# Experts of a two-layer backbone: split token rows, paired scatters, no dummy products, an eighth raw buffer

## The chip, the cores and the metric

The kernel runs on one core of a Trainium2 chip. The time is device microseconds from launch to end of one execution; several executions give a median. TensorE is called PE, VectorE DVE, ScalarE ACT, GpSimd POOL; SP is the engine that issues the loads of the weights.

## The reference

The program is a two-layer backbone for 256 tokens of width 1024. Each layer mixes tokens (short convolution, gated chunks, windowed attention) and then channels. Layer 0's channel mixer is dense; layer 1's is a mixture of experts, which is where the change lies:

```python
def moe_swiglu(h, router, w_gu, w_d):
    logits = jnp.einsum("bld,de->ble", h, router, preferred_element_type=jnp.float32)
    top_v, top_i = lax.top_k(logits, TOP_K)          # 2 of 8 experts for a token
    top_w = jax.nn.softmax(top_v, axis=-1)
    gates = jnp.sum(jax.nn.one_hot(top_i, N_EXPERTS, dtype=jnp.float32) * top_w[..., None], axis=-2)
    y = gates[..., 0:1] * swiglu(h, w_gu[0], w_d[0])
    for e in range(1, N_EXPERTS):
        y = y + gates[..., e:e + 1] * swiglu(h, w_gu[e], w_d[e])
    return y                                          # then x + g2 * y, and a last RMSNorm
```

An expert is 3584 wide: `w_gu[e]` is 1024 x 7168 and `w_d[e]` 3584 x 1024, all fp32.

## The kernel before, in words

**Products in fp32.** Where many tokens share a weight, both factors are split in a high and a low part of a rounded fp32 type (fp32r), and three products high-high, low-high and high-low take the place of one fp32 product. The tile framework records the program in the order of the code, engine by engine, and puts semaphore waits where tiles are shared.

**The token rows.** Ahead of the experts, `token_scale` makes the normalised and modulated rows `tm` (128 tokens x 2 halves x 1024) in four quarters of 512 columns: DVE multiplies from PSUM, POOL adds the shift in place. Between the second and the third quarter DVE works out the tokens' ranks. For an expert, `prep_p` makes a selection matrix P with one 1 a column (its slots: up to 128 for a full block, 64 more on the side), `prep_x` gathers the tokens as products `tm` x P of 192 columns into X (full block, split again in `Xe`; side in `Xo`), `prep_g` scales P by the gates and `prep_t` transposes it for the way back. Expert 0's gather runs ahead of the first weights, those of the others between steps.

**Steps and chunks.** An expert has seven steps of 512 hidden columns, and a table `steps` mixes up to LANES = 3 experts. One step is seven turns of PE: four chunks of gate and up weights (`products`, into PG and PU), the transposition of the gated result (`turned`), two chunks of down weights (`down`, into PY). A chunk is 128 x 2048 fp32, 1 MB, and each is loaded by SP into one of seven raw buffers (raw0 to raw3, mraw, and raw2 and raw4 of the pool `mp`); a load is issued once the buffer's last reader is done.

**Branches by the token counts.** `modes` writes three variants of every turn: full (a 128-token block, 12 split products of 512 columns a chunk), the 64-wide side (fp32 straight from the raw chunk), the 32-wide side. PE reads the counts `full_` and `half_` from registers and branches. With the inputs here experts 0 and 1 have a full block and no side, expert 4 a full block and a 32-wide side, the others only a side. Where a full block has no side, the Else of the inner If issues `idle`: one 8-column product of zeros into the bank of the side. The first eight steps of the table are of experts 0 and 1; their other six alternate with side-only steps.

**Between the steps.** `items` is a table of slots, three a step (`item(3n)` and `item(3n + 1)` ahead of `down`, `item(3n + 2)` behind it), in which one piece of preparation or of scattering is issued. `scatter` brings an expert's result back to the tokens: products of the transposed selection with Y (full) and YO (side) into a bank, which DVE adds to `xt`. In the kernel before a scatter is one token half and one column half, four to an expert.

Of the kernel before, what the change touches and what calls it, by code (L numbers as in the profile page):

```python
# [18 lines left out]
D = 1024  # L19
# [7 lines left out]
NE = 8  # L27
# [109 lines left out]
def backbone_kernel(ctx, tc, xT, small, const, moe_const, gmw, gmb, modk, modd, wa, wg2, wg4, wo, fgu, fd, mgu, mdn, fing, out):  # L137
# [773 lines left out]
    cnt = mo.tile([128, 25], I32, name="cnt")  # L911
    none = mo.tile([128, 8], BF16, name="none")
    before, every = [scr(BF16)[:, 0:128] for _ in range(2)]
    nc.gpsimd.memset(none, 0.0)
    nc.gpsimd.memset(every, 1.0)
# [114 lines left out]
    def prep_p(e):  # L1030

        P = mp.tile([128, 2, NX], F32, name="P")
# [25 lines left out]
    def prep_g(e, bank=None):  # L1058
        P = X[e]["P"]
        for i in range(2):  # L1060
            nc.gpsimd.tensor_scalar(P[:, i, :], P[:, i, :], gates[:, i, e:e + 1], None, op0=OP.mult)  # L1061

    def prep_t(e, bank):

        P = X[e]["P"]
        for s in range(2):
            for i in range(2):
                nc.tensor.transpose(bank[:, s * NX + i * 128:s * NX + (i + 1) * 128], P[:, i, s * 128:(s + 1) * 128], ident)
        X[e]["T"] = pt = mp.tile([128, 2, NX], F32, name="Pt", bufs=LANES + 1)
# [38 lines left out]

    def scatter(e, i, g, bank):

        pt = X[e]["T"]
        ts, gs, hs = slice(i * 128, (i + 1) * 128), slice(g * 512, (g + 1) * 512), slice(64 * g, 64 * g + 64)

        def go(first, last):
            mm(bank, pt[:, 0, ts], X[e]["Y"][:, gs], start=first, stop=last)

        def go_o(first, last):
            mm(bank, pt[hs, 1, ts], X[e]["YO"][hs], start=first, stop=last)  # L1118

# [6 lines left out]
        with c.Else():  # L1126
            go_o(True, True)
        a = xt[:, i, gs]
        post.append(lambda: nc.vector.tensor_tensor(a, a, bank, op=OP.add))  # L1129

    def idle(bank):
        mm(bank[0:8, 0:8], none, none, start=True, stop=True)

    def modes(e, full, half, quarter=None, bank=None):

# [66 lines left out]
    def products(e, j, po):  # L1202
# [25 lines left out]
        modes(e, go, go_o, go_q, po)  # L1228

# [23 lines left out]
    def turned(e, t, po):  # L1253
# [9 lines left out]
        modes(e, turn, turn_o, None, po)  # L1263
        hh, hl = [mp.tile([128, 512], F32R, name=nm) for nm in ("hh", "hl")]
# [8 lines left out]
    def down(e, s, h3):  # L1273
# [4 lines left out]
        for j in range(2):  # L1278
# [22 lines left out]
            modes(e, go, go_o, go_q, PYO)  # L1301
            st.free()


    def scatters(e):
        return [lambda bank, i=i, g=g: scatter(e, i, g, bank) for i in range(2) for g in range(2)]

# [3 lines left out]
    def prep_back(e):  # L1311
        return [lambda bank: prep_g(e), lambda bank: prep_t(e, bank)]

    place(0, [prep_back(0)[0]])
    free = place(3, [prep_back(0)[1]])
    for e in range(1, NE):
# [3 lines left out]
        free = place(max(begin, free), prep(e) + prep_back(e))  # L1320
    for n in range(NE * NS):
        d, ds = steps[n]
        if ds == (NS if d < NE - 1 else TOGETHER) - 1:
            place(3 * n + 5, scatters(d))
    nc.gpsimd.memset(moe_scr("to"), 0.0)
# [38 lines left out]
    def spill(e):  # L1364
        P = mp.tile([128, 2, 64], F32, name="P")
        for i in range(2):
            nc.vector.tensor_scalar(P[:, i, :], slots[:, 0:64], float(SLOTS), rank[:, i, e:e + 1], op0=OP.add, op1=OP.is_equal)
        xs, pt = room[:, :, 0:64], moe_scr("tp")[:, :NX]
        po = PO[0]
        for d in range(KD):  # L1370
            for i in range(2):
                mm(po[:, 0:64], tm[:, i, d * 128:(d + 1) * 128], P[:, i, :], start=i == 0, stop=i == 1)
            nc.vector.tensor_copy(xs[:, d, :], po[:, 0:64])
        for i in range(2):
            mm(po[0:64, 0:1], P[:, i, :], gates[:, i, e:e + 1], start=i == 0, stop=i == 1)
        gs = mp.tile([128, 2], F32, name="gs")
        nc.vector.tensor_copy(gs[0:64, 0:1], po[0:64, 0:1])
        for i in range(2):
            nc.tensor.transpose(PT[0:64, i * 128:(i + 1) * 128], P[:, i, :], ident)
        nc.vector.tensor_copy(pt[0:64, :], PT[0:64, :NX])  # L1380
# [6 lines left out]
        for s in range(NS):  # L1387
# [18 lines left out]
        y, t = [moe_scr(nm) for nm in ("tg", "to")], moe_scr("tu")  # L1406
        for g in range(2):
# [12 lines left out]

    for g in range(2):
        for i in range(2):
            scatter(NE - 1, i, g, (PU, PT, PG, PO[0])[2 * i + g])
        run_post()


    ss = tiny()
    for g in range(2):
# [118 lines left out]
```

## Time and profile before

| what | value |
| --- | --- |
| median of 3 runs | 2087.51 us (2086.2 to 2089.84) |
| profiled execution | 2096.31 us, of which the span of its instructions 2094.2 |
| PE busy | 1922.0 us, 92% of the span |
| DVE, ACT, POOL busy | 62%, 33%, 21% |
| HBM read | 500.55 MB, 240 GB/s over the span |
| PE's mean granted clock | 0.962 of full speed |

The profiled execution is 8.8 us longer than the median of the timed runs. The span falls in a front part up to about 1050 us (layer 0, and layer 1's token mixing), a change-over up to 1088.5 (the router, the token rows, expert 0's gather), the steps up to 2071, and the last norm. Shares over the whole span mix these; the rows below are by stage.

### The profile page before, as it was taken

The numbers are of one execution on the slowest core, as the hardware profiler recorded it, in microseconds if no ns is written. First come the engines' busy times: TensorE is split into PE (matmuls) and PEld (weight loads), VectorE is DVE, ScalarE is ACT, GpSimd is POOL, SyncE is SP. The second block draws the span as 40 slices with busy tenths as digits, with TensorE's granted clock in tenths as the row PEclk, the third lists the DMA queues.
The fourth block names the chain that finished last, engine by engine and source line by source line (L and its number), as shares of the span: only waits on it lengthen the run. The fifth ranks groups of instructions, "written<-read, shape, count | busy, mean of one in ns | idle before, by whom it ended". The sixth has DMA issues, their size and how long they took to land. (4 is left out here: it accounts for less than half of the span.)

```text
span 2094.2 us, 31796 instructions
## 1 busy us (share of the span) xinstructions
PE 1922.0 (92%) x9396; PEld 1304.7 (62%) x9396; DVE 1300.0 (62%) x1946; ACT 695.6 (33%) x903; POOL 445.9 (21%) x188
## 2 busy tenths in 40 slices
PE   7999889989999889899989999998999998898676
PEld 4777668878888668788987765644444444332122
DVE  7488789759967772766568866654454545442222
ACT  4334332332212212554546654433232322210000
POOL 4432234233443325524420000000000000000000
PEclk9999999999999989899999999999999999999888
DMA  6323134424444553433638989999899998899995
GB/s 265 117 67 122 51 126 161 156 90 171 154 148 173 178 192 130 154 104 106 232 123 284 323 304 365 343 376 416 323 370 354 360 365 337 332 389 408 403 387 206
DMA packets 79401, 506.04 MB, mean 242 GB/s; under 512 B 8784, under 2 KB 9424, under 8 KB 28880
## 3 DMA queue, kind: packets, MB, share of 16 engines
q1 hardware_dynamic: 79056, 501.64, 64.1%
q8 instruction: 193, 3.16, 0.6%
q14 instruction: 152, 1.25, 0.2%
HBM read 500.55 MB, written 1.05 MB: 240 GB/s over the span
## 5 line engine op out<-in xcount | busy, mean ns | idle before, releaser
L106 POOL TENSOR_TENSOR w0l<-raw,w0h 128x2048 fp32r<-128x2048 f32 (+6 forms) x43 | 156.0, 3628 | 242.2 <-ACT w0h L102 222.6
L106 POOL TENSOR_TENSOR w1l<-raw,w1h 128x2048 fp32r<-128x2048 f32 (+6 forms) x42 | 153.2, 3649 | 229.4 <-ACT w1h L102 215.5
L1221 PE MATMUL PO<-raw,Xo 128*64 128x512 f32 x768 | 186.3, 620 | 11.3 <-issue 10.0
L226 DVE CUSTOM_DVE_ANT_0 scr<-mraw,crows 128x512 f32<-128x512 f32 x128 | 165.3, 1292 | 40.7 <-DMA mraw<-in_modd_dram 40.6
L1061 POOL TENSOR_SCALAR P<-P,gates 128x256 f32<-128x256 f32 x16 | 22.1, 1392 | 758.4 <-PE PO L1048 622.0
L226 DVE CUSTOM_DVE_ANT_0 scr<-mraw,crows,mcol 128x512 f32<-128x512 f32 x128 | 161.1, 1259 | 4.6
L102 ACT CAST w1h<-raw 128x2048 fp32r<-128x2048 f32 (+3 forms) x82 | 142.2, 1735 | 43.4 <-PE mm L447 22.6
L102 ACT CAST w0h<-raw 128x2048 fp32r<-128x2048 f32 (+3 forms) x82 | 141.2, 1721 | 41.9 <-PE mm L447 28.8
L446 PE MATMUL mm<-Hh,w0h 128*128 128x512 f32 (+1 forms) x380 | 139.1, 376 | 10.7 <-ACT Hh L384 4.2
L446 PE MATMUL mm<-Hh,w1h 128*128 128x512 f32 (+1 forms) x384 | 137.1, 368 | 8.9 <-ACT w1h L102 7.1
L447 PE MATMUL mm<-Hl,w0h 128*128 128x512 f32 (+1 forms) x380 | 137.7, 372 | 6.2 <-POOL Hl L440 6.2
L447 PE MATMUL mm<-Hl,w1h 128*128 128x512 f32 (+1 forms) x384 | 135.6, 364 | 0.0
L1221 PEld LDWEIGHTS PO<-raw,Xo 128*64 128x64 f32 x768 | 55.3, 142 | 115.7 <-issue 114.3
L106 DVE TENSOR_TENSOR w1l<-raw,w1h 128x2048 fp32r<-128x2048 f32 (+3 forms) x49 | 103.5, 2112 | 30.9 <-ACT w1h L102 30.3
L1294 PE MATMUL PYO<-raw,ho 128*64 128x512 f32 x392 | 95.5, 620 | 11.4 <-issue 5.6
L106 DVE TENSOR_TENSOR w0l<-raw,w0h 128x2048 fp32r<-128x2048 f32 (+3 forms) x48 | 97.8, 2037 | 9.7 <-ACT w0h L102 9.0
L106 DVE TENSOR_TENSOR w2l<-raw,w2h 128x2048 fp32r<-128x2048 f32 (+3 forms) x45 | 90.9, 2020 | 19.5 <-ACT w2h L102 12.8
L1236 DVE SCALAR_TENSOR_TENSOR to<-to,PO 64x512 f32<-64x512 f32 x28 | 18.9, 676 | 126.0 <-ACTq L98 78.8
L1270 ACT COPY ho<-PO 128x256 f32<-128x256 f32 x42 | 15.7, 373 | 245.0 <-PE PO L1262 198.8
L449 PE MATMUL mm<-Hh,w0l 128*128 128x512 f32 (+1 forms) x380 | 94.3, 370 | 1.9 <-POOL w0l L106 1.9
L102 ACT CAST w2h<-raw 128x2048 fp32r<-128x2048 f32 (+2 forms) x45 | 81.5, 1811 | 35.6 <-PE PU L1214 26.0
L446 PEld LDWEIGHTS mm<-Hh,w0h 128*128 128x128 f32 x380 | 73.1, 192 | 25.2 <-ACT Hh L384 4.8
(469 smaller groups left out, 4253.9 us busy)
## 6 DMA issues: line engine op xcount, KB each, us to landing
raw<-in_mgu_dram SPq DMA_DIRECT2D x191, 1024.0 KB, 7.9
raw<-in_mdn_dram SPq DMA_DIRECT2D x97, 1024.0 KB, 8.5
mraw<-in_modd_dram SPq DMA_DIRECT2D x80, 512.0 KB, 4.8
mraw<-in_mgu_dram SPq DMA_DIRECT2D x33, 1024.0 KB, 8.1
raw<-in_fgu_dram SPq DMA_DIRECT2D x22, 1024.0 KB, 4.9
raw<-in_wg_dram SPq DMA_DIRECT2D x28, 640.0 KB, 3.9
raw<-in_wa_dram SPq DMA_DIRECT2D x15, 1024.0 KB, 5.0
mraw<-in_mdn_dram SPq DMA_DIRECT2D x15, 1024.0 KB, 7.4
```

Of the source, the lines that this page charges most:

```text
L102: self.nc.scalar.copy(c.hi[:, :n], c.raw[:, :n])
L106: eng.tensor_tensor(c.lo[:, a:b], c.raw[:, a:b], c.hi[:, a:b].bitcast(F32), op=OP.subtract)
L226: nc.vector.tensor_tensor_reduce(scr(), w[:, h * 512:(h + 1) * 512], crows[:, v, h * 512:(h + 1) * 512], scale=1.0, scalar=mcol[:, l, v, i ...
L446: mm(p[:, :n], wh(k), ah(k), start=first and k == ks[0], stop=False)
L447: mm(p[:, :n], wh(k), al(k), start=False, stop=False)
L449: mm(p[:, :n], wl(k), ah(k), start=False, stop=last and k == ks[-1])
L1061: nc.gpsimd.tensor_scalar(P[:, i, :], P[:, i, :], gates[:, i, e:e + 1], None, op0=OP.mult)
L1221: mm(po[64 * g:64 * g + 64], xo[:, kk, :], w[:, k, g, :], start=kk == 0, stop=kk == KD - 1)
L1236: nc.vector.scalar_tensor_tensor(t, t, 1.0, g, op0=OP.add, op1=OP.mult)
L1270: modes(e, split, lambda: nc.scalar.copy(ho, po[:, 0:256]))
L1294: mm(PYO[64 * b:64 * b + 64], ho[:, ff, :], w[:, f, b, :], start=first and ff == 0, stop=last and ff == 3)
```

## The change

It has five parts.

1. `token_scale` ends in two tiles, `tmh` (ACT casts to fp32r) and `tml` (DVE subtracts), in place of `tm`. The gather is then two fp32r products, `tmh` x P and `tml` x P, where it was one fp32 product; P is declared fp32r.
2. `idle` and the Else that called it are gone.
3. A scatter takes both column halves in one branch, into two banks; scatters are placed first, at every third slot from 3n + 6, with the slot behind each kept free, and the preparations fill what is left. Before, preparations came first and four scatters followed from 3n + 5.
4. The scaled selection goes to a scratch tile G and no longer over P.
5. An eighth raw buffer, raw5, and the memory set aside for DMA descriptors becomes 2048 bytes. The last norm's `tm` and the overflow path `spill`, which doesn't run with these counts, are adapted.

```diff
-    tm = mo.tile([128, 2, D], F32, name="tm")
+    tmh, tml = [mo.tile([128, 2, D], F32R, name=nm) for nm in ("tmh", "tml")]
...
-        t, p = tm[:, i, g * 512:(g + 1) * 512], tms[i, g]
+        cs = slice(g * 512, (g + 1) * 512)
+        t, p = scr(), tms[i, g]
         nc.vector.scalar_tensor_tensor(tv, pv_, r[:, i:i + 1], rows[2 + g], op0=OP.mult, op1=OP.mult)
         nc.gpsimd.tensor_tensor(tv, tv, rows[g], op=OP.add)
+        nc.scalar.copy(tmh[:, i, cs], t)
+        nc.vector.tensor_tensor(tml[:, i, cs], t, tmh[:, i, cs].bitcast(F32), op=OP.subtract)
...
-    st.add_raw(mp, ("raw2", "raw4"))
+    st.add_raw(mp, ("raw2", "raw4", "raw5"))
...
-                mm(bank[:, n * NX:n * NX + SLOTS], tm[:, i, (d + n) * 128:(d + n + 1) * 128], P[:, i, 0:SLOTS], start=i == 0, stop=i == 1)
+                for part in (tmh, tml):
+                    mm(bank[:, n * NX:n * NX + SLOTS], part[:, i, (d + n) * 128:(d + n + 1) * 128], P[:, i, 0:SLOTS],
+                       start=i == 0 and part is tmh, stop=i == 1 and part is tml)
...
-            nc.gpsimd.tensor_scalar(P[:, i, :], P[:, i, :], gates[:, i, e:e + 1], None, op0=OP.mult)
+            nc.gpsimd.tensor_scalar(G[:, i, :], P[:, i, :], gates[:, i, e:e + 1], None, op0=OP.mult)
...
-    def scatter(e, i, g, bank):
+    def scatter(e, i, banks):
...
         def go(first, last):
-            mm(bank, pt[:, 0, ts], X[e]["Y"][:, gs], start=first, stop=last)
+            for g in range(2):
+                mm(banks[g], pt[:, 0, ts], X[e]["Y"][:, g * 512:(g + 1) * 512], start=first, stop=last)
...
-    def idle(bank):
-        mm(bank[0:8, 0:8], none, none, start=True, stop=True)
...
-            with tc.If(half_[e] > 0) as c2:
+            with tc.If(half_[e] > 0):
                 side()
-            if bank is not None:
-                with c2.Else():
-                    idle(bank)
...
+    for n in range(NE * NS):
+        d, ds = steps[n]
+        if ds == (NS if d < NE - 1 else TOGETHER) - 1:
+            turn = 3 * n + 6
+            for f in scatters(d):
+                while turn in items:
+                    turn += 3
+                items[turn], items[turn + 1] = f, None
...
-    nc = bacc.Bacc("TRN2", target_bir_lowering=False, num_devices=1)
+    nc = bacc.Bacc("TRN2", target_bir_lowering=False, num_devices=1, dynamic_dma_scratch_size=2048)
```

What the engines' queues hold at three places, from the order of the built programs. First PE, from the last product of the first chunk of gate and up weights to the end of its inner If, before; PO is the bank of the side, `none` the tile of zeros, and the two fours of 64x512 and 32x512 are the sides' products, which are jumped over where there is no side:

```order
L1215 MATMUL PU<-w0l,Xe 128x512
L1147 COMPARE_AND_BRANCH
L1140 COMPARE_AND_BRANCH
L1221 MATMUL PO_8526<-raw_7969,Xo 64x512 [waits DMAHW0_49]
L1221 MATMUL PO_8526<-raw_7969,Xo 64x512 x3
L1140 UNCONDITIONAL_BRANCH
L1227 MATMUL PO_8526<-raw_7969,Xo 32x512 [waits DMAHW0_49]
L1227 MATMUL PO_8526<-raw_7969,Xo 32x512 x3
L1140 UNCONDITIONAL_BRANCH
L1132 LDWEIGHTS none
L1132 MATMUL PO_8526<-none 8x8
L1147 UNCONDITIONAL_BRANCH
```

The same place in the changed program:

```order
L1220 MATMUL PU<-w0l,Xe 128x512
L1155 COMPARE_AND_BRANCH
L1148 COMPARE_AND_BRANCH
L1226 MATMUL PO_8539<-raw_7969,Xo 64x512 [waits DMAHW0_49]
L1226 MATMUL PO_8539<-raw_7969,Xo 64x512 x3
L1148 UNCONDITIONAL_BRANCH
L1232 MATMUL PO_8539<-raw_7969,Xo 32x512 [waits DMAHW0_49]
L1232 MATMUL PO_8539<-raw_7969,Xo 32x512 x3
L1148 UNCONDITIONAL_BRANCH
L1155 UNCONDITIONAL_BRANCH [waits PE_49]
```

The load and the product of `none` are gone, and the unconditional branch that stands in their place waits for PE_49, PE's own semaphore.

Second PE, the end of expert 0's gather, before:

```order
L1048 MATMUL PG<-P,tm 128x192 [waits Pool_49] x2
L1048 MATMUL PG<-P,tm 128x192 x2
L1048 MATMUL PYO<-P,tm 128x192 [waits Activation_49]
L1048 MATMUL PYO<-P,tm 128x192 x3
L1195 TENSOR_LOAD cnt [waits DVE_49,DMAHW2_49,PE_49,DMAHW3_49,Activation_49,Pool_49]
```

And in the changed program, where each product of `tm` has become a pair:

```order
L1050 MATMUL PYO<-P,tmh 128x192 [waits Activation_49]
L1050 MATMUL PYO<-P,tml 128x192
L1050 MATMUL PYO<-P,tmh 128x192
L1050 MATMUL PYO<-P,tml 128x192
L1050 MATMUL PYO<-P,tmh 128x192
L1050 MATMUL PYO<-P,tml 128x192
L1050 MATMUL PYO<-P,tmh 128x192
L1050 MATMUL PYO<-P,tml 128x192
L1200 TENSOR_LOAD cnt [waits DVE_49,DMAHW2_49,PE_49,DMAHW3_49,Activation_49,Pool_49]
```

The count of product instructions doubles, four to eight a bank, each of the same 192 columns.

Third DVE, the token rows, before; lines 980 to 986 are the ranks:

```order
L951 SCALAR_TENSOR_TENSOR tm<-mm,tiny,x 128x512 [waits Activation_49] x2
L980 TENSOR_SCALAR rank<-sel 128x16 [waits DVE_49]
L983 TENSOR_TENSOR rank<-rank,tp 128x16 [waits DVE_49,PE_49]
L984 COPY tiny<-tp 128x8
L985 TENSOR_SCALAR tiny<-tp 128x8
L986 SCALAR_TENSOR_TENSOR rank_h<-tiny,rank 128x16 [waits DVE_49]
L951 SCALAR_TENSOR_TENSOR tm<-mm,tiny,x 128x512 [waits Activation_49]
L951 SCALAR_TENSOR_TENSOR tm<-tp,tiny,x 128x512 [waits Activation_49]
L1160 SCALAR_TENSOR_TENSOR tiny<-tiny 128x8
```

And in the changed program:

```order
L950 SCALAR_TENSOR_TENSOR scr<-mm,tiny,x 128x512 [waits Activation_49]
L953 TENSOR_TENSOR tml<-scr,tmh 128x512 [waits Activation_49]
L950 SCALAR_TENSOR_TENSOR scr<-mm,tiny,x 128x512 [waits PE_49]
L953 TENSOR_TENSOR tml<-scr,tmh 128x512 [waits Activation_49]
L981 TENSOR_SCALAR rank<-sel 128x16 [waits DVE_49]
L984 TENSOR_TENSOR rank<-rank,tp 128x16 [waits DVE_49,PE_49]
L985 COPY tiny<-tp 128x8
L986 TENSOR_SCALAR tiny<-tp 128x8
L987 SCALAR_TENSOR_TENSOR rank_h<-tiny,rank 128x16 [waits DVE_49]
L950 SCALAR_TENSOR_TENSOR scr<-mm,tiny,x 128x512 [waits PE_49]
L953 TENSOR_TENSOR tml<-scr,tmh 128x512 [waits Activation_49]
L950 SCALAR_TENSOR_TENSOR scr<-tp,tiny,x 128x512 [waits PE_49]
```

Behind each quarter's product now stands its own subtraction, which waits for ACT's cast of that quarter, ahead of the ranks and of the next quarter's product.

## Rows read from the trace of the kernel before

**Rows 1.** Busy time, granted clock and DMA by stage; columns in line one.
```profile
core 0: us, PE busy (x) PEld busy (x) DVE busy (x) ACT busy (x) POOL busy (x), PEclk, DMA share, GB/s
1088.50:1248.60 160.10, 158.23 (x712) 118.87 (x711) 129.14 (x110) 98.32 (x81) 8.87 (x6) 1.00 0.84 295
1248.60:1470.00 221.40, 210.56 (x935) 122.68 (x935) 127.45 (x108) 88.42 (x77) 4.11 (x2) 1.00 0.97 373
1470.00:1745.00 275.00, 267.95 (x1312) 128.15 (x1314) 144.58 (x160) 81.89 (x94) 7.30 (x6) 0.99 0.93 355
1745.00:2071.00 326.00, 266.49 (x1238) 96.80 (x1234) 114.62 (x144) 46.15 (x65) 1.84 (x2) 0.91 0.94 373
```

**Rows 2.** Waits of SP's queue, 1088.5 to 2071: total us, times, longest.
```profile
SPq L79 <- PE PO L1132: 166.3, 56, 8.0
```

**Rows 3.** Timeline of PE, end of a chunk: start us, us, instruction.
```profile
1090.94 0.40 PE L1214 MATMUL PU<-w0h,Xe 128*128 128x512 f32 x1
1091.17 0.40 PE L1215 MATMUL PU<-w0l,Xe 128*128 128x512 f32 x1
1091.50 0.17 PE L1132 MATMUL PO<-none 128*8 128x8 bf16 x1
1091.60 0.50 PE L1213 MATMUL PG<-w2h,Xe 128*128 128x512 f32 x1
1091.93 0.39 PE L1214 MATMUL PG<-w2h,Xe 128*128 128x512 f32 x1
```

**Rows 4.** Line 1132 grouped: duration ns min/median/max, first, last start.
```profile
L1132 PEld LDWEIGHTS <-none x98: 82/82/84, 1091.5 to 1469.7; 128*8 128x8 bf16 x98
```

**Rows 5.** PE's sequencer by line, 1088.6 to 1089.72, columns as before.
```profile
L1147 PEldq COMPARE_BRANCH  x2: 174/196/217, 1088.6 to 1088.9; - x2
L98 PEldq COMPARE_BRANCH  x2: 73/121/169, 1089.2 to 1089.3; - x2
L1145 PEldq COMPARE_BRANCH  x1: 73/73/73, 1089.5 to 1089.5; - x1
L1213 PEldq EVENT_SEMAPHORE  x1: 51/51/51, 1089.7 to 1089.7; - x1
```

**Rows 6.** PE's sequencer and weight load, line 1213, 1102.5 to 1103.1.
```profile
L1213 PEldq EVENT_SEMAPHORE  x1: 51/51/51, 1102.9 to 1102.9; - x1
L1213 PEld LDWEIGHTS PG<-w2h,Xe x1: 186/186/186, 1103.0 to 1103.0; 128*128 128x128 f32 x1
```

**Rows 7.** Timelines of ACT, POOL, DVE and PE around the token rows.
```profile
1074.97 0.58 ACT L945 COPY xt<-tp 128x512 f32<-128x512 f32 x1 [0.27 <-PE tp L944]
1076.92 2.48 POOL L952 TENSOR_TENSOR tm<-tm,x 128x512 f32<-128x512 f32 x2 [0.77 <-DVE tm L951]
1077.42 0.79 DVE L1160 SCALAR_TENSOR_TENSOR tiny<-tiny 128x8 f32<-128x8 f32 x1
1081.54 2.56 PE L1048 MATMUL PU<-P,tm 128*128 128x192 f32 x8 [4.70 <-DVE P L1038]
```

**Rows 8.** The same shapes elsewhere, grouped by line.
```profile
L1268 ACT CAST hh<-PT x21: 585/586/592, 1109.9 to 1835.7; 128x512 fp32r<-128x512 f32 x21
L1269 DVE TENSOR_TENSOR hl<-PT,hh x21: 684/692/692, 1110.5 to 1837.8; 128x512 fp32r<-128x512 f32 x21
```

**Rows 9.** Timeline of PE, gather of expert 0, eight records a row.
```profile
1085.90 1.46 PE L1048 MATMUL PG<-P,tm 128*128 128x192 f32 x8
1087.20 1.46 PE L1048 MATMUL PYO<-P,tm 128*128 128x192 f32 x8
```

**Rows 10.** Timeline of PE, fp32r products of 256 columns, ends.
```profile
929.84 0.28 PE L446 MATMUL mm<-Hh,w2h 128*128 128x256 f32 x1
...
931.71 0.28 PE L449 MATMUL mm<-Hh,w2l 128*128 128x256 f32 x1
```

**Rows 11.** PE's waits, 1745 to 2071: total us, times, longest.
```profile
PE PT L1118 <- DVEq L1095: 7.4, 2, 4.4
```

**Rows 12.** One stretch of the last stage, columns as in rows 1.
```profile
1900.00:2000.00 100.00, 75.47 (x344) 21.84 (x344) 24.26 (x36) 6.48 (x13) 0.00 (x0) 0.88 1.00 408
```

More of the change, by code (lines that the diff above doesn't have):

```diff
@@ L1030, in prep_p @@
     def prep_p(e):
-        P = mp.tile([128, 2, NX], F32, name="P")
+        P = mp.tile([128, 2, NX], F32R, name="P")
         side = mp.tile([128, 128], F32, name="side")
@@ L1058, in prep_g @@
     def prep_g(e, bank=None):
-        P = X[e]["P"]
+        P = X[e]["P"].bitcast(F32)
+        X[e]["G"] = G = moe_scr("G").rearrange("p (a b) -> p a b", a=2)
         for i in range(2):
-            nc.gpsimd.tensor_scalar(P[:, i, :], P[:, i, :], gates[:, i, e:e + 1], None, op0=OP.mult)
+            nc.gpsimd.tensor_scalar(G[:, i, :], P[:, i, :], gates[:, i, e:e + 1], None, op0=OP.mult)
     def prep_t(e, bank):
-        P = X[e]["P"]
+        G = X[e]["G"]
         for s in range(2):
             for i in range(2):
-                nc.tensor.transpose(bank[:, s * NX + i * 128:s * NX + (i + 1) * 128], P[:, i, s * 128:(s + 1) * 128], ident)
+                nc.tensor.transpose(bank[:, s * NX + i * 128:s * NX + (i + 1) * 128], G[:, i, s * 128:(s + 1) * 128], ident)
         X[e]["T"] = pt = mp.tile([128, 2, NX], F32, name="Pt", bufs=LANES + 1)
@@ L1107, in scale_last @@
                 nc.vector.tensor_tensor(y[:, bs], PY[:, b, :], g2r[:, bs], op=OP.mult)
-    def scatter(e, i, g, bank):
+    def scatter(e, i, banks):
         pt = X[e]["T"]
-        ts, gs, hs = slice(i * 128, (i + 1) * 128), slice(g * 512, (g + 1) * 512), slice(64 * g, 64 * g + 64)
+        ts = slice(i * 128, (i + 1) * 128)
         def go(first, last):
-            mm(bank, pt[:, 0, ts], X[e]["Y"][:, gs], start=first, stop=last)
+            for g in range(2):
+                mm(banks[g], pt[:, 0, ts], X[e]["Y"][:, g * 512:(g + 1) * 512], start=first, stop=last)
         def go_o(first, last):
-            mm(bank, pt[hs, 1, ts], X[e]["YO"][hs], start=first, stop=last)
+            for g in range(2):
+                hs = slice(64 * g, 64 * g + 64)
+                mm(banks[g], pt[hs, 1, ts], X[e]["YO"][hs], start=first, stop=last)
         with tc.If(full_[e] > 0) as c:
@@ L1127, in scatter, with add, modes @@
             go_o(True, True)
-        a = xt[:, i, gs]
-        post.append(lambda: nc.vector.tensor_tensor(a, a, bank, op=OP.add))
-    def idle(bank):
-        mm(bank[0:8, 0:8], none, none, start=True, stop=True)
-    def modes(e, full, half, quarter=None, bank=None):
+        def add():
+            for g in range(2):
+                a = xt[:, i, g * 512:(g + 1) * 512]
+                nc.vector.tensor_tensor(a, a, banks[g], op=OP.add)
+        post.append(add)
+    def modes(e, full, half, quarter=None):
         def side():
@@ L1227, in go_q @@
                     mm(po[a:a + 32], xo[:, 2 * j + k, 0:32], w[:, k, g, :], start=j == 0, stop=j == 3, tile_position=(0, a))
-        modes(e, go, go_o, go_q, po)
+        modes(e, go, go_o, go_q)
     def gated(e, po):
@@ L1262, in turn_o @@
                 nc.tensor.transpose(po[:, k * 64:(k + 1) * 64], to[0:64, k * 128:(k + 1) * 128], ident[0:64, 0:64])
-        modes(e, turn, turn_o, None, po)
+        modes(e, turn, turn_o)
         hh, hl = [mp.tile([128, 512], F32R, name=nm) for nm in ("hh", "hl")]
@@ L1300, in go_q @@
                         mm(PYO[a:a + 32], ho[:, 2 * j + f, 0:32], w[:, f, b, :], start=first and j == 0, stop=last and j == 1, tile_position=(0, a))
-            modes(e, go, go_o, go_q, PYO)
+            modes(e, go, go_o, go_q)
             st.free()
     def scatters(e):
-        return [lambda bank, i=i, g=g: scatter(e, i, g, bank) for i in range(2) for g in range(2)]
+        return [lambda bank, i=i: scatter(e, i, (bank, PT)) for i in range(2)]
     def prep(e):
@@ L1320, in backbone_kernel @@
         free = place(max(begin, free), prep(e) + prep_back(e))
[L1321 to L1324, printed above, removed]
     nc.gpsimd.memset(moe_scr("to"), 0.0)
@@ L1364, in spill @@
     def spill(e):
-        P = mp.tile([128, 2, 64], F32, name="P")
+        P = mp.tile([128, 2, 64], F32R, name="P")
         for i in range(2):
             nc.vector.tensor_scalar(P[:, i, :], slots[:, 0:64], float(SLOTS), rank[:, i, e:e + 1], op0=OP.add, op1=OP.is_equal)
-        xs, pt = room[:, :, 0:64], moe_scr("tp")[:, :NX]
+        xs, pt = room[:, :, 0:64], moe_scr("gq")[:, :NX]
         po = PO[0]
@@ L1371, in spill @@
             for i in range(2):
-                mm(po[:, 0:64], tm[:, i, d * 128:(d + 1) * 128], P[:, i, :], start=i == 0, stop=i == 1)
+                for part in (tmh, tml):
+                    mm(po[:, 0:64], part[:, i, d * 128:(d + 1) * 128], P[:, i, :], start=i == 0 and part is tmh, stop=i == 1 and part is tml)
             nc.vector.tensor_copy(xs[:, d, :], po[:, 0:64])
         for i in range(2):
-            mm(po[0:64, 0:1], P[:, i, :], gates[:, i, e:e + 1], start=i == 0, stop=i == 1)
+            mm(po[0:64, 0:1], P[:, i, :].bitcast(F32), gates[:, i, e:e + 1], start=i == 0, stop=i == 1)
         gs = mp.tile([128, 2], F32, name="gs")
@@ L1378, in spill @@
         for i in range(2):
-            nc.tensor.transpose(PT[0:64, i * 128:(i + 1) * 128], P[:, i, :], ident)
+            nc.tensor.transpose(PT[0:64, i * 128:(i + 1) * 128], P[:, i, :].bitcast(F32), ident)
         nc.vector.tensor_copy(pt[0:64, :], PT[0:64, :NX])
@@ L1405, in spill @@
                         mm(PY[0:64, b, :], h[:, 2 * j + f, :], w[:, f, b, :], start=s == 0 and j == 0 and f == 0, stop=s == NS - 1 and j == 1 and f == 1)
-        y, t = [moe_scr(nm) for nm in ("tg", "to")], moe_scr("tu")
+        y, t = [moe_scr(nm) for nm in ("tg", "to")], moe_scr("G")
         for g in range(2):
@@ L1419, in backbone_kernel @@
                 spill(e)
[L1421 to L1424, printed above, removed]
+    for i in range(2):
+        scatter(NE - 1, i, ((PU, PT), (PG, PO[0]))[i])
+    run_post()
+    tm = mp.tile([128, 2, D], F32, name="Xe", bufs=LANES)
     ss = tiny()
```

2 lines of the change are left out of this document (removed).

## Prediction

> **What bounds the kernel now.** I read the page's slices first, then a table of the last part by stage, then the chain and waits at the edges of those stages. The experts fill the last half. [rows 1] is to be read in two columns, TensorE's (PE's) busy time against the length of the stage, and the DMA share. From 1088.5 to 1248.6 us PE is busy 158.23 of 160.10 us and the DMA share is 0.84: PE is the bound. From 1248.6 to 1470 PE is idle 221.40 - 210.56 = 10.8 us at a DMA share of 0.97: nearly both. From 1470 to 1745 PE is idle 7 us. From 1745 to 2071 PE is idle 59.5 us at 373 GB/s, and the weights are the bound. [rows 2] says who holds the weight stream: SP's queue waits 166.3 us for the dummy products of line 1132 that write PO, that is for PE to be done with a chunk. So a microsecond added to PE ahead of 1470 comes out at the end; one added behind 1745 mostly does not.
>
> The first eight steps of the table belong to experts 0 and 1, which have full blocks only, as have six of the steps up to 1470: 14 steps of 7 chunks, and indeed the dummy ran 98 times [rows 4]. 8 x 7 = 56 of them lie in the first stage, 42 in the second.
>
> **The dummy products.** [rows 3] shows the end of a chunk: products start 0.23 us apart (1090.94, 1091.17), then the dummy starts 0.33 later, and the next chunk's first product 0.10 after it at 1091.60, followed by the next at 0.33 instead of 0.23. Against an unbroken stream the dummy costs 0.10 + 0.10 + 0.10 = 0.30 us, 98 times 29 us. But what stands in its place is no unbroken stream. The order shows an unconditional branch on PE that waits for PE's own count, the one that the chunk's last product raises. Until now PE's sequencer ran ahead of the array: it stood at a wait of line 1213 at 1089.7 [rows 5], 1.5 us before the running chunk's last product started. Now it must stop until that product has ended; only then does it walk the branches to the next chunk.
>
> One such stop, from the start of the last product: that product lasts 0.40 us [rows 3]; a semaphore wait is 0.05, the last line of [rows 5]; the branches from the closing one to the next chunk's wait run from 1088.9 to 1089.7, 0.8 us [rows 5]; from that wait to the first product of a chunk 0.1, with the wait at 1102.9 and the weights loaded from 1103.0 [rows 6]. That is 1.35 us; at three of seven boundaries further empty branches (gate, turn of h) add about 0.5 by the same rows, 0.2 on average: 1.55, of which some 0.1 may already lie ahead of the wait. Before, the next chunk began 1091.60 - 1091.17 = 0.43 us after the last product. I take 1.0 us each, 98 us. Nothing hides the first 56, since PE has 1.9 us to spare there; of the other 42 the stage's 10.8 us idle can take at most that. **+86 us.**
>
> Bounds: with the shortest branch of [rows 5], 0.073, four times in place of 0.8, a stop is 0.40 + 0.05 + 0.29 + 0.10 - 0.43 = 0.41, 40 us, less 10.8 is +29. With the branches at 1.3 everywhere it is 1.42, 139 us, +128. Below both lies that the wait costs nothing, rival A. I take the middle, since the rows of 0.8 are those of this very path. [...]
>
> **Splitting the tokens.** Each quarter of the token rows now goes VectorE (DVE) product, GpSimd (POOL) add, ScalarE (ACT) cast, DVE subtraction, and in the new order the subtraction stands right behind its own product, ahead of the next quarter's. DVE's queue is in order, so the add and the cast are waited out four times. An add is 2.48 / 2 = 1.24 us [rows 7], a cast of this shape 0.59, a subtraction 0.69 [rows 8]: 4 x 2.52 = 10.1 us, with hand-overs 10.4. Behind it stand DVE's counts and the selection matrix P of expert 0, and PE waits for P now already (from 1081.54 back 4.70 us [rows 7]), so it is all on the path. The first cast also stands behind ACT's fourth copy, which ends as late as 1074.97 + 0.58 = 1075.55 [rows 7]; for that I allow 0.6. Off go about 2 us, since the adds no longer run beside DVE's small operations (line 1160 takes 0.79 us for 128x8 [rows 7]), and 2 in the first gather: its 32 records take from 1081.54 to 1087.20 + 1.30, 7.0 us [rows 7, 9], and 117/163 of that, as worked out below, is 5.0. **+7 us**, bounds 3 to 13.
>
> **The gather.** An fp32 product of 192 columns shows as two records; eight records take 1087.20 - 1085.90 = 1.30 us, 163 ns each [rows 9]. Now there are as many records, each an fp32r product of 192 columns. No such product under 256 columns is in the trace; at 256 they are 0.117 us apart (929.84 to 931.71, 16 of them [rows 10]), at 512 0.232 [rows 3]. By the nearest row 117 ns: experts 1 to 6 have 32 records each, 192 x 46 ns = **-9 us**. Proportional to columns it would be 88 ns, -14; at the fp32 product's whole price, 326 ns, it is +31, and +4 more for expert 0 (rival B). Expert 7's lies where the weights bound. [...]
>
> **One more raw buffer.** SP may run one chunk further ahead when PE's stage ends: 1.05 MB at 373 GB/s is 2.8 us less to fetch in the last stage [rows 1], and a little in jitter. **-4 us**, at most the 17.8 us of PE idle ahead of 1745.
>
> **The scatters.** Two halves share one branch and the next slot stays free. PE waited 7.4 us for DVE at line 1118 in the last stage [rows 11], but that stage has 59.5 us of PE idle: **-1 us**, bounds 0 and -7. The scaling into a matrix of its own is POOL work of the same size, hidden where POOL is busy 9 of 160 us [rows 1].
>
> **Sum.** 86 + 7 - 9 - 4 - 1 = +79 on the profiled execution's 2096.3: 2175. That execution is 8.8 us over the median of the runs, 2087.5, so the forecast is **2166 us**.
>
> **Rivals.**
> A, the other side: the wait costs nothing, because PE's sequencer overlaps it with the products in flight, and the dummy's 0.30 us is gained. For it speaks that a wait by itself is 0.05 us [rows 5]; against, that this one opens only at the product's end and has the walk of branches behind it. It decides where a stop adds under about 0.05 us over the dummy's chunk end. -29 + 7 - 9 - 4 - 1 = -36: 2051.
> B, the stops as forecast and the split gather at the price of an fp32 product for each half: +31 + 4 in place of -9: 2210. For it: fp32r under 256 columns is not seen; against: an fp32 product of 192 already takes two records at 163.
> C, cheap stops: PE waits out the product but walks the branches at the fast end, +29: 2166 - 57 = 2109.
> [...]
> E, no change: the stops hide behind the weights. At 0.84 of DMA in the first stage that can't be, short of the weights slowing by themselves.
>
> **How the numbers follow.** Chances: forecast 0.47, A 0.12, B 0.14, C 0.14, D 0.10, E 0.03. The range must leave out no more than 0.2: it runs from just under C to beyond D, 2100 to 2230 us, which leaves out A, E and those cases where B and D meet. The likeliest case's own range, from its bounds and the smaller terms, is 2130 to 2200. A measurement of this kernel tells about 0.2% from no change. Faster is A, 0.13 with a little of C where the bounds add; same is E, 0.03; the rest, 0.84, is slower.
>
> **What would show it.** Right: the first product of each full-only chunk starts 1.2 to 1.6 us after the last of the chunk before; the stage of the eight full-only steps takes about 215 us in place of 160 with PE idle some 55; a stretch of PE gathers shows 32 records 0.09 to 0.12 apart; P of expert 0 is ready some 9 us later than now against the token statistics; the stage behind 1745 keeps its length. Wrong: a full-only stage under 165 us (A), gather records 0.3 us apart (B), a granted clock under 0.95 before 1470 (D), or the wait as no more than 0.4 us (C).

## The result and the profile after

| kernel | median | against before |
| --- | --- | --- |
| before | 2091.96 us (6 runs) | 1 |
| changed | 2210.98 us (6 runs) | 1.0571, 95% interval 1.0535 to 1.0607 |

The change costs 119 us, 112 to 127 by the interval. The forecast was 79 more (2166, range 2100 to 2230). The profiled spans are 2094.2 and 2209.5 us, 115.3 apart. Two executions far above the others of their kernel, one of e10 below (9,252 us) and one of the kernel before beside e5 to e8 (2,208 us), are left out of the ratios.

The stages of the changed kernel, cut at the events of [rows 1], except that the third cut comes 103 of PE's products earlier, so that the last two stages are read together:

```profile
core 0: us, PE busy (x) PEld busy (x) DVE busy (x) ACT busy (x) POOL busy (x), PEclk, DMA share, GB/s
1093.70:1317.50 223.80, 158.28 (x658) 115.88 (x658) 132.41 (x112) 98.95 (x81) 7.50 (x8) 0.97 0.63 214
1317.50:1594.50 277.00, 214.68 (x888) 121.72 (x888) 127.54 (x105) 89.42 (x77) 1.89 (x2) 0.96 0.83 297
1594.50:1855.00 260.50, 249.30 (x1209) 116.51 (x1208) 134.90 (x146) 77.87 (x89) 7.49 (x4) 0.98 0.92 351
1855.00:2186.00 331.00, 267.45 (x1342) 100.13 (x1344) 122.61 (x157) 49.96 (x71) 1.89 (x2) 0.95 0.96 382
```

The first stage grew from 160 to 224 us with the same 158 us of PE work in it, the second from 221 to 277; the two behind them together went from 601 to 591. All the loss lies where full-only steps run, nearly all of it as idle PE, and the weights' rate fell to 214 GB/s in the first of the two stages. The queue of SP says who holds the loads now, with 346 us on the new branch where [rows 2] has the dummy:

```profile
SPq L79 <- PEq L1155: 345.9, 84, 7.4
```

PE at the end of the first chunk, to be read against [rows 3]:

```profile
1096.12 0.40 PE L1219 MATMUL PU<-w0h,Xe 128*128 128x512 f32 x1
1096.36 0.40 PE L1220 MATMUL PU<-w0l,Xe 128*128 128x512 f32 x1
1097.88 0.47 PE L1218 MATMUL PG<-w2h,Xe 128*128 128x512 f32 x1 [1.13 <-issue]
1098.19 0.40 PE L1219 MATMUL PG<-w2h,Xe 128*128 128x512 f32 x1
```

From the last product to the next chunk's first it is 1.52 us, where it was 0.43. What PE's sequencer does in between, by line (the counterpart of [rows 5]):

```profile
L1155 PEldq EVENT_SEMAPHORE  x1: 51/51/51, 1096.8 to 1096.8; - x1
L1155 PEldq COMPARE_BRANCH  x1: 174/174/174, 1097.0 to 1097.0; - x1
L98 PEldq COMPARE_BRANCH  x2: 73/124/174, 1097.3 to 1097.4; - x2
L1153 PEldq COMPARE_BRANCH  x1: 73/73/73, 1097.6 to 1097.6; - x1
L1218 PEldq EVENT_SEMAPHORE  x1: 51/51/51, 1097.8 to 1097.8; - x1
L1218 PEld LDWEIGHTS PG<-w2h,Xe x1: 186/186/186, 1097.9 to 1097.9; 128*128 128x128 f32 x1
```

The wait opens at 1096.8, when the product that began at 1096.36 ends; then come four branches, the wait of the next chunk at 1097.8 and its weights at 1097.9: 1.0 us of walking. In [rows 5] the same branches ran while products were still in flight. The wait is executed as often as the dummy was [rows 4]:

```profile
L1155 PEldq EVENT_SEMAPHORE  x98: 51/51/51, 1096.8 to 1594.7; - x98
```

The token rows on DVE's timeline, and expert 0's gather on PE's:

```profile
1070.12 0.75 DVE L950 SCALAR_TENSOR_TENSOR scr<-mm,tiny,x 128x512 f32<-128x512 f32 x1
1073.43 0.69 DVE L953 TENSOR_TENSOR tml<-scr,tmh 128x512 fp32r<-128x512 f32 x1 [2.57 <-ACT tmh L952]
1074.04 0.75 DVE L950 SCALAR_TENSOR_TENSOR scr<-mm,tiny,x 128x512 f32<-128x512 f32 x1
```

```profile
1087.14 0.50 PE L1050 MATMUL PU<-P,tmh 128*128 128x192 f32 x1 [13.09 <-DVE P L1039]
1087.43 0.41 PE L1050 MATMUL PU<-P,tml 128*128 128x192 f32 x1
1087.65 0.41 PE L1050 MATMUL PU<-P,tmh 128*128 128x192 f32 x1
...
1092.53 0.27 PE L1050 MATMUL PYO<-P,tml 128*128 128x192 f32 x1
...
1093.20 0.27 PE L1050 MATMUL PYO<-P,tml 128*128 128x192 f32 x1
```

DVE waits 2.57 us between the first product and its subtraction, and 2.09, 2.02 and 2.02 in the other three quarters, with nothing of the next quarter in between. PE stands 13.09 us before the gather, where it stood 4.70 [rows 7]. The last seven records are (1093.20 - 1092.53) / 6 = 0.112 us apart, where [rows 9] has 0.163, and in the later gathers 0.112 is the median. But the first 24 of expert 0's 32 records are 0.213 us apart: from 1087.1 to 1092.3 the granted clock is 0.50. The kernel before also has slow records there, ten at 0.32 us, at a granted clock of 0.56 from 1081.5 to 1084.8, before it comes to 0.163.

### The profile page after: what moved, and what is told of

Same layout as the page of the kernel before. It is cut to its first block, busy times and chain, and to the rows that moved or that the text cites. A ratio compares the mean times of both kernels' runs of the same rounds, so it can differ in the third digit from the quotient of the medians.

```text
span 2209.5 us, 31575 instructions
## 1 busy us (share of the span) xinstructions
PE 1902.3 (86%) x9298; PEld 1285.5 (58%) x9298; DVE 1304.5 (59%) x1950; ACT 699.1 (32%) x907; POOL 443.0 (20%) x187
## 5 line engine op out<-in xcount | busy, mean ns | idle before, releaser
L1226 PE MATMUL PO<-raw,Xo 128*64 128x512 f32 x768 | 191.4, 628 | 28.9 <-issue 25.5
L226 DVE CUSTOM_DVE_ANT_0 scr<-mraw,crows 128x512 f32<-128x512 f32 x128 | 158.2, 1236 | 37.8 <-DMA mraw<-in_modd_dram 37.5
L1065 POOL TENSOR_SCALAR G<-P,gates 128x256 f32<-128x256 f32 x16 | 18.8, 1182 | 800.3 <-DVE P L1039 791.2
L226 DVE CUSTOM_DVE_ANT_0 scr<-mraw,crows,mcol 128x512 f32<-128x512 f32 x128 | 169.7, 1326 | 4.6
L102 ACT CAST w0h<-raw 128x2048 fp32r<-128x2048 f32 (+3 forms) x85 | 146.7, 1726 | 69.2 <-PE mm L447 28.7
L446 PE MATMUL mm<-Hh,w0h 128*128 128x512 f32 (+1 forms) x380 | 140.2, 379 | 10.8 <-ACT Hh L384 4.2
L106 DVE TENSOR_TENSOR w0l<-raw,w0h 128x2048 fp32r<-128x2048 f32 (+3 forms) x51 | 104.7, 2054 | 34.3 <-ACT w0h L102 34.0
```

What stands on the lines that cost most here:

```text
L102: self.nc.scalar.copy(c.hi[:, :n], c.raw[:, :n])
L106: eng.tensor_tensor(c.lo[:, a:b], c.raw[:, a:b], c.hi[:, a:b].bitcast(F32), op=OP.subtract)
L226: nc.vector.tensor_tensor_reduce(scr(), w[:, h * 512:(h + 1) * 512], crows[:, v, h * 512:(h + 1) * 512], scale=1.0, scalar=mcol[:, l, v, i ...
L446: mm(p[:, :n], wh(k), ah(k), start=first and k == ks[0], stop=False)
L1065: nc.gpsimd.tensor_scalar(G[:, i, :], P[:, i, :], gates[:, i, e:e + 1], None, op0=OP.mult)
L1226: mm(po[64 * g:64 * g + 64], xo[:, kk, :], w[:, k, g, :], start=kk == 0, stop=kk == KD - 1)
```

## The experiments

Each kernel was timed beside the kernel before. Of each profile three stretches are given: A from the third full product of the first chunk to the first product of a side (the eight full-only steps), B from there to the last product of the 84th full chunk (the end of the full-only steps), C from there to the end. All are in microseconds, read from the starts of PE's products.

```
kernel                             median  ratio (95%)              A      B      C
before                             2092.0  1                      159.5  220.8  624.8
changed                            2211.0  1.0571 (1.0535-1.0607) 223.2  276.7  615.3
e1 changed, dummies back           2085.4  0.9961 (0.9939-0.9984) 157.2  216.1  620.8
e2 before, dummies gone            2222.4  1.0628 (1.0582-1.0675) 225.2  280.7  625.3
e3 42 stops left                   2152.5  1.0290 (1.0241-1.0340) 190.0  249.4  618.0
e4 before, buffer alone            2093.9  1.0002 (0.9984-1.0020) 159.5  216.9  633.5
e5 products in both arms           2144.5  1.0238 (1.0164-1.0313) 148.4  227.0  669.3
e6 before, scatters alone          2082.6  0.9953 (0.9933-0.9972) 159.5  217.0  616.1
e7 changed, one more If            2235.8  1.0685 (1.0636-1.0733) 240.2  278.9  619.3
e8 e1, one more If                 2089.5  0.9974 (0.9955-0.9992) 156.7  215.7  626.3
e9 e1, subtractions last           2077.2  0.9933 (0.9909-0.9957) 157.4  215.5  609.3
e10 e1, dummies in fp32r           2078.4  0.9921 (0.9894-0.9947) 152.2  209.6  618.9
e13 e1, longer jump                2309.3  1.1051 (1.1012-1.1091) 163.4  269.6  776.9
e12 e9 and e10 together            2069.1  0.9887 (0.9863-0.9911) 152.5  210.0  615.8
```

**The dummies, back and alone.** e1 puts the Else and its product back into the changed kernel; e2 takes them from the kernel before, with nothing else; e3 puts them back in the gate and up chunks only.

```diff
-            with tc.If(half_[e] > 0):
+            with tc.If(half_[e] > 0) as c2:
                 side()
+            if bank is not None:
+                with c2.Else():
+                    idle(bank)
```

> The changed kernel with the dummy products back at all three places (98 executed). Theory (the stops): in the two traces the way from a full chunk's last product to the next product grew from 0.44 to 1.60 us at 84 places and from 0.31 to 2.03 at the 14 turns of h, 97 + 24 = 121 us, which is all of the 119 us lost; so this kernel takes the time of before within some 10 us, 2080 to 2100, the other parts together being worth -10 to +5. Rival (much of the loss is the new order of scatters and preparations, the split rows or the extra buffer, the stops are worth the 86 us that I forecast): about 2125.

> The kernel before without its dummy products and with nothing else changed. Theory: 2092 + 121 less what the second stage can absorb, at most 10.8, so 2200 to 2213, and the stage of the eight full-only steps grows from 160 to about 222 us. Rival (86 us for the stops): 2178. Second rival (the dummies are a mere cost and go for nothing): 2062.

> The changed kernel with the dummy products back in the gate and up chunks alone: 42 stops are left, 28 behind chunks of down weights and 14 behind the turns of h. Theory (each stop counts by itself): 14 x 1.72 + 28 x 1.16 = 57 us over the kernel with all dummies, about 2145. Rival (stops hide behind one another or behind the weights, so that the last ones cost most or nothing): under 2110 or over 2180.

e1 came out at 2085, a little under before; e2 at 2222, above the 2200 to 2213 expected, with A at 225. So taking away 98 dummies alone accounts for the whole loss and 12 us more, and the rest of the change is a gain of 8 us (3 to 13). e3 has 2152 where 2145 stood. Its 21 stops in A cost 190.0 - 157.2 = 32.8 us over e1, the 21 in B 33.3, 1.6 each, so stops add up one by one and hide nowhere; the rivals of e1 and e3 are out. The 42 ways from a last product to the next grew by 60 us of these 66. The second rival of e2, that a dummy is a mere cost, is out by 160 us.

The windows of e1 at A and B show what the stops had taken: PE is busy all but 2.7 us of A again, and the clock is 1.00 where the changed kernel had 0.97 and 0.96.

```profile
1094.70:1252.60 157.90, 155.23 (x712) 115.66 (x710) 129.26 (x110) 98.34 (x81) 14.54 (x8) 1.00 0.86 299
1252.60:1469.00 216.40, 207.94 (x934) 120.35 (x933) 126.90 (x107) 88.21 (x77) 2.31 (x3) 1.00 0.98 380
```

This pair differs in the dummies alone, so its rows part the loss. From e1 to the changed kernel PE's idle time in the two stretches rises from 11 to 128 us; its busy time rises too, from 363 to 373 us, though 98 small products are gone. So about 10 us of the loss are products that take longer at the lower granted clock. The other kernels with stops show a lower clock there as well (A and B of e2 0.98 and 0.96, of e3 0.97 and 0.96, of e7 0.93 and 0.97), while the kernel before has 1.00 in both. e2 against the kernel before gives the same 10 us (PE busy 368 and 377), which its theory had left out.

**What a stop is made of.** e7 adds an If that is never taken, behind each gate and up chunk of the changed kernel; e8 adds it to e1.

```diff
         modes(e, go, go_o, go_q)
+        with tc.If(half_[e] > 5):
+            nc.scalar.copy(extra, extra)
```

> The changed kernel with one more If that is never taken (its body is a small copy on ScalarE) behind each chunk of gate and up weights, so that PE walks one empty branch more to the next chunk. Theory (a stop's price is the walk of branches behind the wait): a walk's step is 0.25 to 0.3 us by the rows of the sequencer, 56 x 0.27 = 15 us over the changed kernel, about 2226, and the way from a chunk's last product to the next grows by that much in the trace. Rival (the price is the array's restart or the semaphore, and the sequencer's branches are overlapped): 2211.

> The same extra If in the changed kernel with its dummy products, where nothing stops PE's sequencer. Theory: the sequencer is a chunk ahead, the walk is hidden, 2085 within 5 us. Rival (a branch costs wherever it stands): 2100.

Behind a stop the If costs 1.0685 - 1.0571, 1.1% or 24 us; where nothing stops, 2089.5 against 2085.4, inside both intervals, with A and B within 0.5 us of e1's. So this If is free as long as PE's sequencer is ahead, and is paid behind a wait. The end of a gate and up chunk in e7:

```profile
1101.51 0.39 PE L1223 MATMUL PU<-w2l,Xe 128*128 128x512 f32 x1
1103.19 0.47 PE L1221 MATMUL PG<-w1h,Xe 128*128 128x512 f32 x1 [1.29 <-issue]
```

1.68 us here; on average over the 56 full-only chunks of gate and up weights 1.80 against 1.53 in the changed kernel, the 0.27 that was expected. 56 x 0.27 is 15 us of the 24. The clock accounts for most of the other 9: A, where 32 of these chunk ends make 9 us, grew by 17, and PE was busy 166.0 us in it at a granted clock of 0.93, where the changed kernel has 157.7 at 0.97. (ScalarE, which has the copy, also walks the If, and that was not tried apart.)

**The branch without stop or dummy.** e5 writes the full products in both arms of the inner If, for the turns on PE alone, so that a product ends each arm (shortened).

```diff
         with tc.If(full_[e] > 0) as c:
-            full()
-            with tc.If(half_[e] > 0):
+            with tc.If(half_[e] > 0) as c2:
+                full()
                 side()
+            with c2.Else():
+                full()
```

> The changed kernel with neither dummy nor stop: where a chunk has a full block, the full products are written in both arms of the inner If, with the side behind them in one, so that the last product itself raises the count and no branch waits. Theory: the stops (121 to 128 us) are gone, and so is the dummy's 0.30 us, 56 x 0.30 = 17 us in the first stage and at most 13 in the second, where the weights may take some: 2085 less 17 to 29, 2056 to 2068. Rival (the dummy's 0.33 and 0.33 us are the price of the branch itself or of the chunk's change, not of the small product): 2085. Second rival (4,000 more product instructions on PE cost in loading code): over 2090.

In A the theory held: the stream is unbroken across the chunk's end, and A takes 148.4 us, 8.8 less than with dummies.

```profile
1098.51 0.40 PE L1227 MATMUL PU<-w0l,Xe 128*128 128x512 f32 x1
1098.74 0.40 PE L1225 MATMUL PG<-w2h,Xe 128*128 128x512 f32 x1
```

But B lost 11 us and C 48, and the kernel came out 59 us over e1. The second rival held in that more product instructions cost, and mostly where they are not executed. C has no full-only chunk left; there PE's side-only steps branch past the full products, and they now stand twice in the way. e13 tests that: e1 with the full products a second time in an arm that is never taken (shortened, again for PE's turns alone).

```diff
-                side()
+                with tc.If(half_[e] > 5) as c4:
+                    full()
+                    side()
+                with c4.Else():
+                    side()
```

> The changed kernel with its dummy products, and with the full products written a second time in an arm that is never taken, so that PE executes the same and the code that side-only steps jump over has the length of the kernel with products in both arms. Theory: that kernel lost 48 us behind the last full-only chunk because long jumps stop PE's sequencer (45 branches over 1 us there against 28, 185 against 123 us in all); so this one keeps the first stage (157 us) and loses 30 to 50 us in the last: 2115 to 2135. Rival (the loss comes from something else in that kernel, as the weights' stream at 337 in place of 364 GB/s): 2085.

By this edit the side stands once more too. In a chunk of gate and up weights a side-only step of e13 jumps over 41 products, where e5 has 32 and e1 21, so the jump is longer than e5's and not, as expected above, of the same length.

The time is 2309, far over what was expected; C is 777 us, and B, in which side-only steps alternate with full-only ones, is 54 us over e1's. The row of C among the stages of e5 and of e13; e1 has 600.00 us, 524.10 of them PE, at a clock of 0.95 and 364 GB/s.

```profile
1472.00:2121.00 649.00, 536.61 (x2566) 219.20 (x2564) 259.18 (x303) 128.69 (x159) 9.38 (x6) 0.93 0.90 337
```

```profile
1529.70:2287.00 757.30, 577.58 (x2564) 231.69 (x2565) 259.60 (x303) 128.53 (x159) 9.38 (x6) 0.87 0.81 290
```

The outer branch of `modes` on PE's sequencer in C, in e1, e5 and e13 (min/median/max ns):

```profile
L1158 PEldq COMPARE_BRANCH  x318: 65/208/4193, 1469.7 to 2065.4; - x159
```

```profile
L1153 PEldq COMPARE_BRANCH  x318: 65/208/4828, 1472.7 to 2117.6; - x159
```

```profile
L1158 PEldq COMPARE_BRANCH  x319: 65/208/5668, 1527.8 to 2283.8; - x160
```

PE executes the same products in all three in C. The median branch stays at 208 ns, but the longest grow, and there are more of them: of the branches on PE behind 1090 us, 52 take over 1 us in e1, 91 in e5 and 148 in e13, and all branches together take 457, 579 and 762 us. So code that is only jumped over costs, and mainly where side-only steps jump. Of the 157 us between the rows of e13 and e1, 53 are busy time of PE, at a clock of 0.87 in place of 0.95. What the instruction queue loads over the execution grows too, 3.16, 3.62 and 4.55 MB in e1, e5 and e13 (1.56 and 1.87 in C of the first two); that the loading makes the long branches is not shown, for no run here varied the distance of one jump alone. Against e1, e13 lost nearly four times as much as e5 (224 and 59 us). Its longer jump, the dummies that e5 does without, and expert 4's chunks, which jump too, all point that way; how much each of them makes was not tried.

**The other parts alone.** e4 adds two lines of the change to the kernel before, the eighth buffer and the smaller descriptor memory; e6 adds only part 3, the paired and moved scatters, with all lines of the diff that lie in `scatter`, `scatters` and the placing. Of e6's lines (shortened):

```diff
-        return [lambda bank, i=i, g=g: scatter(e, i, g, bank) for i in range(2) for g in range(2)]
+        return [lambda bank, i=i: scatter(e, i, (bank, PT)) for i in range(2)]
...
-            place(3 * n + 5, scatters(d))
```

> The kernel before with the eighth raw buffer and the smaller descriptor memory alone. Theory: one chunk more ahead of the last stage, -4 us, 2088. Rival one: more depth takes away all of PE's waits before 1745, -18, 2074. Rival two: the descriptor memory or the changed addresses cost, slower than 2096.

> The kernel before with the paired and moved scatters alone. The changed kernel with dummies was 0.39% under before, 8 us, and the buffer alone gave nothing. Theory: those 8 us are the split gather (-9) and the token rows (+5 by the trace) and so the scatters give the rest, some -4: 2091. Rival (as forecast, the scatters give 1 us or nothing, and the gather more than I made of it): 2094 to 2095.

The buffer gives nothing (0.9984 to 1.0020). The scatters give 0.47%, 10 us, as much as e1 as a whole (0.39%), so the rest of e1 is about nothing on balance. PE's waits at the scatters' products sum to 3.0 us from 1700 us on in e6, where the kernel before has 15.0 from 1710 on, 7.4 of them in [rows 11]. But all of PE's waits there fall only from 59.7 to 56.2 us, since those at the sides' products grow, and C differs by some 9 us between profiles (633.5 in e4). So where the 10 us lie isn't settled.

**Two repairs and the best version.** e9 issues the four subtractions behind the last quarter's product; e10 makes the dummy's tile fp32r instead of bf16; e12 is both.

```diff
-        nc.vector.tensor_tensor(tml[:, i, cs], t, tmh[:, i, cs].bitcast(F32), op=OP.subtract)
+        rest.append(lambda: nc.vector.tensor_tensor(tml[:, i, cs], t, tmh[:, i, cs].bitcast(F32), op=OP.subtract))
...
+    for f in rest:
+        f()
     front_stack.close()
```

```diff
-    none = mo.tile([128, 8], BF16, name="none")
-    nc.gpsimd.memset(none, 0.0)
+    none = mo.tile([128, 8], F32R, name="none")
+    zero = mo.tile([128, 8], F32, name="zero")
+    nc.gpsimd.memset(zero, 0.0)
+    nc.gpsimd.tensor_copy(none, zero)
```

> The changed kernel with its dummy products, and with the four subtractions of the token rows issued together behind the ranks and the last quarter's product, so that the adds and casts of one quarter run beside DVE's work on the next. Theory: a quarter's round of product, add, cast and subtraction takes 3.4 us in the trace and DVE stands idle 2.0 to 2.5 us of it, four times; with the subtractions last only the last add and cast are waited for, so expert 0's gather starts 5 to 7 us earlier and the time is 2079 where the kernel with dummies has 2085. Rival (the steps' front is bound by the first weights or by ACT): 2085.

> The changed kernel with its dummy products, these of the products' own type (fp32r) in place of bf16. Theory: a bf16 dummy costs 0.30 us because its weights, and those of the product behind it, are loaded in front of their products and not beside the one before; with one type the weights go in beside the running product, a dummy costs 0.1, and 56 x 0.2 = 11 us are gained in the first stage and as much as the weights let through in the second: 2070 to 2075. Rival (the price is that of a small product by itself, or of the change of bank): 2085, no change.

> The changed kernel with dummy products of type fp32r and with the four subtractions last, the two edits that each gained by themselves (0.9933 and 0.9921 of before, where the kernel with bf16 dummies has 0.9961). Theory: they lie in different stages and add up, 0.9961 - 0.0028 - 0.0040 = 0.989, some 2070. Rival (a microsecond taken from PE ahead of 1470 no longer comes out at the end, since the weights bound the last stage): 0.992 to 0.993.

In e9 the subtractions run in one piece and the gather starts 10.9 us after the first token product (1070.78), where the changed kernel took 17.0 and the kernel before 8.7. The median is 8 us under e1's, though the two intervals overlap. First DVE, then PE:

```profile
1070.78 1.60 DVE L954 SCALAR_TENSOR_TENSOR scr<-mm,tiny,x 128x512 f32<-128x512 f32 x2
...
1075.38 4.18 DVE L957 TENSOR_TENSOR tml<-scr,tmh 128x512 fp32r<-128x512 f32 x4
```

```profile
1081.70 0.50 PE L1056 MATMUL PU<-P,tmh 128*128 128x192 f32 x1 [6.16 <-DVE P L1045]
```

In e10 the dummy slips in behind the last product, and the next chunk follows at once:

```profile
1097.18 0.40 PE L1230 MATMUL PU<-w0l,Xe 128*128 128x512 f32 x1
1097.41 0.17 PE L1147 MATMUL PO<-none 128*8 128x8 f32 x1
1097.44 0.48 PE L1228 MATMUL PG<-w2h,Xe 128*128 128x512 f32 x1
1097.76 0.39 PE L1229 MATMUL PG<-w2h,Xe 128*128 128x512 f32 x1
```

From the last product to the next chunk's second it is 0.58 us; an unbroken stream has 0.46, and the bf16 dummy of [rows 3] 0.76. So at this place it costs 0.12 in place of 0.30. Its weights load from 1097.18, beside the last product, where those of the bf16 dummy load at 1091.50, as it starts. A and B fell by 5.0 and 6.5 us, half of what was expected in the first stage: over the 53 places in A the way to the next product fell by 0.11 on average. e10's interval overlaps e1's too; e12, which has both, is clear of it, came out as its theory had it, and is the fastest kernel of the study, 1.13% under before.

## Why the prediction was right, and where its terms were off

The measured 2211 us lies in the range, but above the 2130 to 2200 that I gave the likeliest case. In number it is nearer to rivals B (2210) and D (2216: a granted clock of 0.88 as in [rows 12] would make the 369 us of products ahead of 1470 [rows 1] an estimated 369 x 0.12 / 0.88 = 50 us longer) than to the forecast; it is the traces that tell them apart.

**The stops.** The mechanism was the one forecast: the trace has the stop, its four pieces and their order, and e1 and e2 show that it is the whole loss, together with the fall of the clock that comes with it. The term was too small: 98 x 1.0 less 10.8 is 87, where I wrote 86, and the traces hold 121 before any cover. Counted over all 98 places, the way from the last product to the next is 1.53 us on average (median 1.41) at the 56 gate and up chunks, which is what the pieces of [rows 3, 5, 6] gave, but 1.74 at the 28 down chunks and 2.03 at the 14 turns of h; before it was 0.45, 0.43 and 0.31. 56 x 1.08 + 28 x 1.31 + 14 x 1.72 = 121. I had given every stop the price of the first kind, and rounded it down.

**The cover.** The 10.8 us idle of the second stage [rows 1] were to take as much off. Of the 121 us 62 belong to 53 stops in A, which grew by 63.7, and 59 to 45 in B, which grew by 55.9. PE's idle time in B away from the stops did shrink, from 10.8 to 4.2 us, and DMA's share fell from 0.97 to 0.83. That step came true in part, but most of it was lost again: at a clock of 0.96 PE was busy 4.4 us longer in B, with fewer products. The sum had no term for that; it stood in rival D alone. At the 11 places where a side's product with a chunk's weights follows a stop, the way is longest, 2.37 us against 0.38: I read that as PE's longer jumps over the full products, hidden until then, coming into the open as well, but no run tries it apart.

**The token rows.** Forecast +7. The gather starts 17.0 us after the first token product, not 8.7, so 8.3 later, and is shorter by 0.8 (1087.14 to the last record at 1093.20, 6.2 us against 7.0): +7.5. Right in sum; the gather was to be 2 shorter, which left out that 24 of its 32 records run at a granted clock of 0.50, 0.213 us apart.

**The gather.** The price of a record was right at full clock: 0.112 us, where I took 0.117 from 256 columns, so rival B is out. The count was not: I took 192 records ahead of the weights' stage, but of the experts' 224 only 112 lie before the end of B, 64 in A and 48 in B. 112 x 0.051 is 5.7 us in place of 9, and A of e1 shows 2.3 of them.

**The buffer** gave nothing in place of 4 us: B of e4 is 3.9 us shorter than before, but C 8.7 longer, and nothing of it reached the end. **The scatters** gave 10 (6 to 14) in place of 1, the middle beyond my bound of 7. I had PE's waits in the last stage covered by the weights; whether that step failed, or the gain lies elsewhere, stays open, as the profile of e6 doesn't place it.

With 121 for the stops, about -7 for the cover and about +10 for the clock, 7.5, -6, 0 and -10 the sum is some +115, which is what the spans say. The +10 and -7 are read from pairs that differ in the dummies, e1 and changed, before and e2, and the -10 comes from medians, so the close fit is partly luck.

**The rivals.** A and E are out with e1 and e2; C by the way of 1.52 us; B by the record. D came in part: the clock fell from 1.00 to 0.97 and 0.96 in the two stages, between the forecast's 1.00 and D's 0.88, and cost about 10 us where D had 50. In the first stage PE's busy time stayed at 158 us although the dummies were gone and the records shorter.

## What to carry to other kernels

A runtime branch on an engine, PE here, was free only while that engine's sequencer was ahead of its work: the same added If cost 24 us where stops stood ahead of it (e7) and 4 us, inside both intervals, where none did (e8). In the changed program the arm that has nothing to do ends in a branch that waits for PE's own count, 98 times, and the 1.0 us of walking to the next work was paid behind the wait. Look in the order of the built program for branches that wait on their own engine, and give such an arm the cheapest instruction that can carry the count, of the type of its neighbours (0.12 us in fp32r, 0.30 in bf16); writing the work in both arms also ended the wait, but the longer code was paid where it is jumped over (48 us in C of e5). And where an engine's clock falls when it stands idle between products, as PE's did here (from 1.00 to 0.97 and 0.96, about 10 us), count that beside the wait.

## What the runs showed of the hardware

- A small product costs 0.30 us between fp32r products when it is bf16 [rows 3] and 0.12 when it is fp32r (e10, at the chunk ends shown). The fp32r one's weights load beside the product ahead (from 1097.18 in e10), the bf16 one's don't (1091.50 in the kernel before).
- An fp32r product of 192 columns takes 0.112 us at a granted clock of 1.00, one of 256 columns 0.117: nearly the same, so the time doesn't follow the columns here. At 0.50 the one of 192 takes 0.213.
- With PE idle for 128 us of A and B, most of it at 98 chunk ends, its granted clock was 0.97 and 0.96 there, where in e1, with 11 us idle, it was 1.00; PE's busy time rose by 10 us.
- A compare-and-branch has a median of 0.18 us on PE, 0.04 on ScalarE and 0.05 on VectorE (line 1155 of the changed kernel, 329 on each). PE's has a tail up to 5.7 us in e13, and the tail grew with the code that is jumped over (4.2, 4.8 and 5.7 us in e1, e5 and e13).
